# The prompt's values computed with the tokens on the output partitions, and first of all products

## The chip, the cores and the metric

The kernel runs on one core of one Trainium2 chip. The metric is the device time of one launch in microseconds; lower is better. Three runs of the kernel before were timed, and a fourth was profiled.

## The reference

One layer of a decoder step on two groups of tokens: a prompt of 512 new tokens and 8 running sequences of 4 tokens each (32 "sample" tokens, each sequence with 4096 cached positions in pages of 128). All arithmetic is fp32. Cut to what matters here:

```python
glu_a, glu_b, q, k, v, g_conv, g_att = jnp.split(x @ w_in, cuts, axis=-1)   # 512,512,512,512,512,1024,1024 columns
u = glu_a * sigmoid(glu_b)
c, new_conv = causal_depthwise_conv(u, past_conv, conv_w, conv_b)           # 31 taps, 512 channels
conv_out = silu(layer_norm(c)) @ w_conv_proj
o = stick_breaking_attention(q, concat(past_k, k), concat(past_v, v), ...)  # 8 heads of 64
mixed = (sigmoid(g_conv) * conv_out + sigmoid(g_att) * (o @ w_att_proj)) @ w_out
x = layer_norm(ALPHA * x + mixed)
# then a SwiGLU FFN, a gated per-layer embedding and a second layer_norm
return x, k, v, new_conv                                                    # k and v of all new tokens are outputs
```

## The kernel before

Activations lie channels first: `x` is 8 blocks of 128 channels by 544 tokens (512 of the prompt, 32 of the samples). Every fp32 operand of a product is split into a high and a low part (`split`, line 275: a rounded copy `xh` or `wh`, mostly by ScalarE, and the rest `xl` or `wl` by VectorE or GpSimd), and a product is three: high x high, low x high, high x low (`passes`, line 464). Weights come in units of 512 KB (`w_load`, line 340), 8 blocks of 128 x 128 each; a unit is split in two halves into four rotating buffers, so that a half can only be split when a half of four back has been used. The raw units of q and k (`FIRST`, line 1721) lie in slots of their own, since the sample tokens need them whole and early; all others share three rotating buffers `wr`.

The order of the work is not written by hand. `main` (line 1110) is the main stream of products; beside it run streams as Python generators: the loader and splitter of weights, the prefetch of cache pages on SP's queue (17 slots of 512 KB at most), the scores and sums over the cache (`scores`, `decode`, lines 673 and 694; 32 chunks, with tiles `kv`, `z`, `dz`, `dl`, `dp`, `av`), the prompt's attention (`pa_pair`, line 780; tiles `pa`, `pb`, 12 pairs), the depthwise convolution on VectorE (`conv`, line 868; 31 steps for each of four channel blocks, tile `c`, and sums over channels `tot`), and norms. A planner (`Weave`, line 64) with a clock for each engine decides at build time which stream issues next, by costs written in the code. What it emits is a fixed order for each engine, and on the chip each engine follows it strictly, waiting where an operand is late.

The main stream first goes through the 20 units of `ORDER` (line 1720): q, k, b, a, v of the first 128 output channels, then of the second, and so on. The weights are the stationary operand and x moves, so the result has channels on the partitions and tokens along the row. For q and k only the 512 prompt tokens move (one product of 512 columns); for b, a and v all 544 move as two products of 272. After b and a comes the gated `u`, which starts that block's convolution. v is the odd one: attention needs it with tokens on the partitions, so `vt` is copied out of PSUM (line 1209), stored, transposed in four 128 x 128 pieces by TensorE through the bank `tp` and copied to `v` by VectorE (`back`, line 1216), and then two more pieces with the samples' tokens go through the same bank to `vs` (`sample`, line 1224). The bank `tp` is shared with the transposes of the scores (`dz`), of the prompt's weights (`pa`) and with half of the prompt's scores. At the very start `first_sample` (line 1075) computes q and k of the 32 sample tokens from the raw units of `FIRST` (`z<-wq,xr`) and transposes them (`a_s`); `decode` then prepares the new tokens' part (`anew`), and only after that do the cache chunks start.

After the 20 units come the attention and convolution gates (`ga`, `gc`, 8 units each), the two projections (`ohl`, `sh`), the output projection (`m`) with the first norm in two halves of 256 tokens, and then the FFN; its second part, with 288 columns, needs the finished sample rows `r_s` that `sample_tail` (line 966) makes once all cache chunks are through.

Of the kernel before, what the change touches and what calls it, by code (L numbers as in the profile page):

```python
# [175 lines left out]
def step_kernel(ctx: ExitStack, tc: tile.TileContext, xT, pT, ck, cvv, state, pt, W, cv, cc, yT, kT, vT, cvo):  # L176
# [195 lines left out]
    def loader():  # L372
        for u in range(NU):
            if u in FIRST:
                continue
            if u in AGAIN:
                yield lambda: AGAIN[u] in kept
                raw[u] = kept.pop(AGAIN[u])
                continue
            if u in SLOTTED:  # L380
                yield lambda: u * 8 <= cur["pos"] + 8 * WAHEAD
            elif u in PAIR and u == PAIRS[PAIR[u]][1]:
                yield lambda: u * 8 <= cur["pos"] + 40 and cur["wp"] < 3
            else:
                yield lambda: u * 8 <= cur["pos"] + 32 and cur["raw"] < 3
            w_load(u)
# [307 lines left out]
    def decode():  # L694
        yield on(qblk, ks)
        for r in range(2):
# [17 lines left out]
            V.tensor_copy(out=anew[:, r, 112:128], in_=zb[:, :16])  # L714
# [65 lines left out]
    def pa_pair(idx, m, tiles):  # L780
# [55 lines left out]
        for i, c, w in seg:  # L836
            for kt in range(i + 1):
                for r, (zb, l) in zip(rows, ab):
                    mm(0.125, pa["o"][r, 128 * i:128 * i + 128], v_sb[m][:, kt * 128 + r.start:kt * 128 + r.stop],
                       l[:, c + kt * 128:c + (kt + 1) * 128], kt == 0, kt == i)  # L840
# [269 lines left out]
    def main():  # L1110
# [7 lines left out]
        raw[0] = slot("wq", (128, 1024))  # L1118
# [12 lines left out]
        for u in FIRST[1:]:  # L1131
# [4 lines left out]
        wv.add(first_sample(list(xr), dict(raw)), 2)  # L1136
# [35 lines left out]
        vs = v2 = None  # L1172
        wv.add(prompt_attention(), 2)
        wv.add(conv(), 3)
        for w, m in ORDER:
            o = []
# [29 lines left out]
            else:  # L1206
                yield spare(1)
                vt = tmp("vt")
                S.activation(out=halves(vt), in_=p[:, :, :HT], func=AF.Copy)
                wv.when(on(vt), lambda m=m, vt=vt: store(vT[m], vt))  # L1210
                if m % 2 == 0:
                    v2 = slot("v", (128, 2, 512))
                if m == 0:
                    vs = slot("vs", (128, 2, 512))

                def back(m=m, vt=vt, v2=v2):
                    yield wv.bank("tp")
                    tp = bank("tp")
                    for kt in range(4):
                        tr(tp[:, kt * 128:(kt + 1) * 128], vt[:, kt * 128:kt * 128 + 128])  # L1220
                    V.tensor_copy(out=v2[:, m % 2], in_=tp)
                    v_sb[m] = v2[:, m % 2]

                    def sample():
                        yield wv.bank("tp")
                        tp = bank("tp")
                        for r in range(2):
                            tr(tp[:, r * 128:(r + 1) * 128], vt[:, 400 + 16 * r:528 + 16 * r])
                        V.tensor_copy(out=vs[:, :, m * 128:(m + 1) * 128],
                                      in_=tp[:, :256].rearrange("p (r c) -> p r c", r=2))  # L1230
                        drop()
                        if m == 3:
                            v_sb["vs", 0], v_sb["vs", 1] = vs[:, 0], vs[:, 1]
                    wv.when(on(v2), sample)
                wv.when(on(vt), back)
# [484 lines left out]
ORDER = [(w, m) for m in range(4) for w in "qkbav"]  # L1720
# [13 lines left out]
def layout(d):  # L1734
# [15 lines left out]
    q, k, v = _units(wi[:, 1024:1536]), _units(wi[:, 1536:2048]), _units(wi[:, 2048:2560])  # L1750
# [31 lines left out]
OUTS = {"yT": (8, 128, 544), "kT": (4, 128, 544), "vT": (4, 128, 544), "cvo": (4, 128, 302)}  # L1782


def unlayout(r):
# [6 lines left out]
    vp, vs = tok(r["vT"])  # L1792
# [23 lines left out]
```

## Time and profile before

| | us |
|---|---|
| median of three runs | 994.26 |
| lowest, highest | 992.68, 996.72 |
| the profiled execution | 997.66 |
| its span | 995.9 |
| TensorE busy (products) | 950.5 (95%) |
| TensorE weight loads busy | 830.8 (83%) |
| VectorE busy | 782.9 (79%) |
| ScalarE busy | 538.5 (54%) |
| GpSimd busy | 177.7 (18%) |
| moved by DMA | 222.00 MB, mean 223 GB/s |

The engines are PE (TensorE), PEld (its weight loads), DVE (VectorE), ACT (ScalarE), POOL (GpSimd) and SP (the queue that issues nearly all loads). A line such as L238 or L146 is that of a helper through which all products or all vector operations go, so tiles are told apart by name: `g<-xh,wh` is a product into the bank `g` with `xh` moving and `wh` stationary. In a row that groups instructions stand the count, then the busy time in us, the mean ns of one, and the idle time of the engine just before them with what ended it. In a row in order of time stand the start and the duration in us. Busy time of a product covers its way through the array, so the spacing of starts, not the mean duration, says what one costs in a run of them.

### The profile page before, as it was taken

What the parts mean: (1) busy time and instruction counts of PE and PEld (TensorE: products, weight loads), DVE (VectorE), ACT (ScalarE), POOL (GpSimd) and SP (SyncE); (2) the same over time, 40 slices, a digit from 0 to 9 for tenths busy, and PEclk for the clock granted to TensorE, in tenths of its full rate; (3) what the DMA queues carried; (4) which work ended last, traced back from release to release, by engine and by line L of the source; (5) the groups of instructions that cost most, each with busy time, mean ns of one, the idle gap of its engine ahead of it and who ended that gap; (6) DMA issues with size and microseconds to landing.
All of it is one profiled execution on the core that took longest, in us unless ns stands there. A gap on an engine that the chain in (4) does not pass through costs nothing.

```text
span 995.9 us, 22464 instructions
## 1 busy us (share of the span) xinstructions
PE 950.5 (95%) x7998; PEld 830.8 (83%) x7998; DVE 782.9 (79%) x1287; ACT 538.5 (54%) x1041; POOL 177.7 (18%) x156
## 2 busy tenths in 40 slices
PE   8989998999899999999999879999999999999995
PEld 7866566668777797688878779999999999999994
DVE  4798898999965666466688786999999999943366
ACT  4634666576786786244467554554554555622224
POOL 1230323313111102033343240000000000220020
PEclk9999999999999999999999889999999999999997
DMA  9949999999979999999999634223223221222302
GB/s 356 343 158 305 339 309 333 316 318 313 328 257 322 314 347 345 331 335 356 321 324 369 248 109 178 96 86 117 96 86 126 87 85 65 86 105 85 128 1 90
DMA packets 101393, 222.00 MB, mean 223 GB/s; under 512 B 11169, under 2 KB 14498, under 8 KB 101282
## 3 DMA queue, kind: packets, MB, share of 16 engines
q1 hardware_dynamic: 99410, 217.46, 62.5%
q10 hardware_dynamic: 1872, 3.11, 0.8%
q8 instruction: 63, 1.03, 0.4%
q14 instruction: 48, 0.39, 0.1%
HBM read 215.45 MB, written 5.07 MB: 221 GB/s over the span
## 4 chain that ended last, share of the span: by engine, by line
PE 73%; DVE 14%; DMA 6%; issue 3%; ACT 2%; SPq 2%; POOL 0%; ACTq 0%; DVEq 0%; POOLq 0%
PE g L238 43%; PE z L238 10%; PE av L238 8%; PE o L238 5%; DVE c L146 5%; PE tp L238 4%; DMA kv<-in_ck 3%; DVE pb L146 2%; PE tp L243 1%; DMA wr<-in_W 1%; SPq L228 1%; DVE dl L146 1%; SPq L657 1%; DVE pa L146 1%; DVE dz L146 1%
## 5 line engine op out<-in xcount | busy, mean ns | idle before, releaser
L146 ACT ACTIVATE wh<-wr 128x512 fp32r<-128x512 f32 x236 | 147.0, 628 | 202.9 <-PE g L238 100.7
L146 DVE TENSOR_TENSOR wl<-wr,wh 128x512 fp32r<-128x512 f32 x190 | 133.1, 705 | 51.7 <-ACT wh L146 42.9
L146 POOL TENSOR_TENSOR wl<-wr,wh 128x512 fp32r<-128x512 f32 x50 | 82.0, 1645 | 493.8 <-ACT wh L146 455.7
L238 PE MATMUL g<-xh,wh 128*128 128x272 f32 (+1 forms) x512 | 127.4, 320 | 0.6 <-ACT wh L146 0.6
L238 PE MATMUL g<-h,wh 128*128 128x272 f32 x704 | 122.3, 290 | 0.0
L238 PE MATMUL g<-xl,wh 128*128 128x272 f32 (+1 forms) x512 | 119.3, 305 | 0.8 <-DVE xl L146 0.8
L238 PE MATMUL g<-xh,wl 128*128 128x272 f32 (+1 forms) x512 | 119.1, 304 | 0.7 <-POOL wl L146 0.7
L146 DVE SCALAR_TENSOR_TENSOR c<-u,cvt,c 128x512 f32<-128x512 f32 x120 | 113.1, 943 | 3.3
L238 PEld LDWEIGHTS g<-h,wh 128*128 128x128 f32 x704 | 103.1, 189 | 0.3
L238 PEld LDWEIGHTS g<-xh,wh 128*128 128x128 f32 x512 | 83.3, 192 | 22.3 <-issue 17.8
L238 PEld LDWEIGHTS g<-xl,wh 128*128 128x128 f32 x512 | 83.7, 191 | 3.6 <-DVE xl L146 1.5
L238 PEld LDWEIGHTS g<-xh,wl 128*128 128x128 f32 x512 | 83.3, 191 | 3.7 <-POOL wl L146 1.0
L238 PE MATMUL g<-h,wl 128*128 128x272 f32 x352 | 80.1, 289 | 0.0
L146 ACT ACTIVATE wh<-wq 128x512 fp32r<-128x512 f32 x87 | 54.5, 629 | 39.6 <-PE g L238 28.7
L238 PE MATMUL g<-x1h,wh 128*128 128x272 f32 (+2 forms) x216 | 65.0, 301 | 5.4 <-ACT x1h L146 4.8
L238 PE MATMUL z<-kv,qblk 128*32 128x256 f32 x1024 | 65.5, 382 | 2.6 <-DMA kv<-in_ck 2.6
L238 PE MATMUL g<-x1h,wl 128*128 128x272 f32 (+2 forms) x216 | 63.4, 294 | 0.0
L238 PE MATMUL g<-x1l,wh 128*128 128x272 f32 (+2 forms) x216 | 63.4, 293 | 0.0
L146 DVE TENSOR_TENSOR wl<-wq,wh 128x512 fp32r<-128x512 f32 x75 | 54.7, 734 | 10.9 <-ACT wh L146 9.8
L238 PE MATMUL av<-kv,dp 128*32 128x512 f32 x512 | 63.2, 608 | 0.0
L146 ACT ACTIVATE pa<-pa 128x384 f32<-128x384 f32 (+1 forms) x96 | 52.5, 555 | 17.3 <-DVE pa L146 15.8
L238 PEld LDWEIGHTS g<-h,wl 128*128 128x128 f32 x352 | 58.1, 188 | 0.0
(316 smaller groups left out, 2352.1 us busy)
## 6 DMA issues: line engine op xcount, KB each, us to landing
kv<-in_ck SPq DMA_DIRECT2D x256, 256.0 KB, 4.4
kv<-in_cvv SPq DMA_DIRECT2D x256, 256.0 KB, 5.3
wr<-in_W SPq DMA_DIRECT2D x98, 512.0 KB, 3.9
wq<-in_W SPq DMA_DIRECT2D x37, 512.0 KB, 5.0
wa<-in_W SPq DMA_DIRECT2D x12, 512.0 KB, 10.2
xr<-in_xT SPq DMA_DIRECT2D x8, 272.0 KB, 5.0
out_yT<-pw SPq DMA_DIRECT2D x6, 272.0 KB, 2.3
out_kT<-qk ACTq DMA_DIRECT2D x4, 272.0 KB, 5.5
```

What stands on the lines that cost most here:

```text
L146: fn(**kw)
L228: eng.dma_start(out=out, in_=in_)
L238: T.matmul(out, lhsT=lhsT, rhs=rhs, start=start, stop=stop)
L243: T.transpose(out, in_, ident)
L657: reg[col] = nc.sync.value_load(ptt[0:1, col:col + 1], min_val=0, max_val=POOL - 1)
```

## The change

The values leave the shared loop and get a function of their own, `values`. There the roles are exchanged: for each of the 8 channel blocks, x is the stationary operand (128 channels by 128 tokens) and the weights move (512 columns, all value channels at once). Five accumulations run side by side, four for the prompt's 512 tokens and one for the last 128 tokens, of which 32 are the samples' and 96 the prompt's again; they take both double banks `g` and the bank `o`. The results have tokens on the partitions and are copied out of PSUM as they are, by VectorE or ScalarE (`evac`), and stored; there are no transposes and no `vt`. The output array's layout and its reading back change with it, and so do the places where the samples' own weights stand in `anew` (96 + 16 r in place of 112).

`ORDER` now has the four value units first, then b, a, q, k for each channel block. So the first unit comes through the shared buffers `wr`, the next two are loaded ahead of q and k, and the fourth, b0 and a0 behind them.

```diff
-            if u in FIRST:
+            if u in FIRST or u < 3:
...
-            V.tensor_copy(out=anew[:, r, 112:128], in_=zb[:, :16])
+            V.tensor_copy(out=anew[:, r, 96 + 16 * r:112 + 16 * r], in_=zb[:, :16])
...
-                    mm(0.125, pa["o"][r, 128 * i:128 * i + 128], v_sb[m][:, kt * 128 + r.start:kt * 128 + r.stop],
+                    mm(0.125, pa["o"][r, 128 * i:128 * i + 128], v_sb[m][kt][:, m * 128 + r.start:m * 128 + r.stop],
...
-        raw[0] = slot("wq", (128, 1024))
+        raw[0] = big.tile([128, 1024], F32, tag="wr", bufs=3, name="wr")
+        cur["raw"] += 1
...
-        for u in FIRST[1:]:
+        for u in (1, 2, *FIRST):
             w_load(u)
...
-        vs = v2 = None
+        def values():
+
+            yield room()
+            p = [gps()]
+            yield room()
+            p.append(gps())
+            yield wv.bank("o")
+            out = [p[t // 2][:, t % 2] for t in range(4)] + [bank("o")]
+            cols = [slice(128 * t, 128 * t + 128) for t in range(4)] + [slice(NT - 128, NT)]
...
+            for k in range(8):
...
+                w, x = hl[divmod(pos // 4, 2)], xin(k)
+                yield on(*w, *x)
+                for t in range(5):
+                    for i, (a, b) in enumerate(((x[0], w[0]), (x[1], w[0]), (x[0], w[1]))):
+                        mm(0.2305, out[t], a[:, cols[t]], b, k == 0 and i == 0, k == 7 and i == 2)
+                    yield
...
+            v = [slot("v", (128, 2, 512)) for i in range(2)] + [slot("vs", (128, 512))]
+            v = [v[t // 2][:, t % 2] for t in range(4)] + [v[2]]
+            for t in range(5):
+                evac(v[t], out[t])
...
         for w, m in ORDER:
+            if w == "v":
+                if m == 0:
+                    yield from values()
+                continue
...
-                vt = tmp("vt")
-                S.activation(out=halves(vt), in_=p[:, :, :HT], func=AF.Copy)
-                wv.when(on(vt), lambda m=m, vt=vt: store(vT[m], vt))
...
-                def back(m=m, vt=vt, v2=v2):
-                    yield wv.bank("tp")
-                    tp = bank("tp")
-                    for kt in range(4):
-                        tr(tp[:, kt * 128:(kt + 1) * 128], vt[:, kt * 128:kt * 128 + 128])
-                    V.tensor_copy(out=v2[:, m % 2], in_=tp)
...
-ORDER = [(w, m) for m in range(4) for w in "qkbav"]
+ORDER = [("v", m) for m in range(4)] + [(w, m) for m in range(4) for w in "baqk"]
...
-OUTS = {"yT": (8, 128, 544), "kT": (4, 128, 544), "vT": (4, 128, 544), "cvo": (4, 128, 302)}
+OUTS = {"yT": (8, 128, 544), "kT": (4, 128, 544), "vT": (5, 128, 512), "cvo": (4, 128, 302)}
```

How this moves instructions is told by the order on each engine. First TensorE at the place where the first cache scores (`z<-kv`) stand. Before, they come in b1, the eighth unit (`g_955`), behind q1 and k1 (`g_903`) and behind the first block's value transposes:

```order
L243 MATMUL tp_941<-cct_65,anew_73 128x128
L238 MATMUL g_903<-xh_132,wh_817 128x512
L238 MATMUL g_903<-xl_133,wh_817 128x512
L238 MATMUL g_903<-xh_132,wl_818 128x512
L238 MATMUL g_955<-xh_126,wh_851 128x272 x2
L238 MATMUL g_955<-xl_127,wh_851 128x272 x2
L238 MATMUL g_955<-xh_126,wl_852 128x272 x2
L238 MATMUL z_963<-kv_134,qblk_68 32x256
```

Now, in b0 (`g_664`), the first unit behind the values:

```order
L243 MATMUL tp_710<-cct_65,anew_73 128x128
L238 MATMUL g_664<-xh_136,wh_490 128x272 x2
L238 MATMUL g_664<-xl_137,wh_490 128x272 x2
L238 MATMUL g_664<-xh_136,wl_491 128x272 x2
L238 MATMUL g_664<-xh_138,wh_490 128x272 x2
L238 MATMUL g_664<-xl_139,wh_490 128x272 x2
L238 MATMUL g_664<-xh_138,wl_491 128x272 x2
L238 MATMUL z_727<-kv_140,qblk_68 32x256
```

The cache scores have moved from the eighth unit of the main stream to the one that follows the values; ahead of them stand the values' 120 products and most of b0 in place of q0, k0, b0, a0, v0, q1 and k1.

Second VectorE at the start of the convolution (`c`). Before, in its first channel block, the copies of the transposed values stand between its steps:

```order
L146 COPY v_823<-tp_869 128x512
L146 SCALAR_TENSOR_TENSOR c_135<-u_538,cvt_64,c_135 128x512 x4
L146 COPY vs_824<-tp_912 128x2x128
L146 SCALAR_TENSOR_TENSOR c_135<-u_538,cvt_64,c_135 128x512 x4
L146 COPY anew_73<-tp_941 128x128
```

Now the same block begins behind a0's gate (`u`), with the scan chain of a cache chunk (`dp`, `dl`, `dz`, `cnew`) in that place:

```order
L146 TENSOR_TENSOR u_764<-g_773,sg_767 128x8x4
L146 TENSOR_SCALAR c_141<-u_764,cvt_64 128x512
L146 SCALAR_TENSOR_TENSOR c_141<-u_764,cvt_64,c_141 128x512 x3
L146 TENSOR_SCALAR dp_985<-dz_799 128x256
L146 SCALAR_TENSOR_TENSOR dl_800<-dl_800,cnew_74,dp_985 128x256
L146 TENSOR_TENSOR dz_799<-dz_799,dl_800 128x256
L146 COPY cnew_74<-dl_800 128x1
L146 SCALAR_TENSOR_TENSOR c_141<-u_764,cvt_64,c_141 128x512 x14
```

The copies out of `tp` are gone from among the steps, `anew` is finished ahead of the convolution, and the first two chunks' scans now stand ahead of it or just behind its first steps.

Third TensorE in the first FFN part, at the last of the sample tokens' sums (`sq_s`) and the first product that needs the finished sample rows (288 columns). Before, 12 products stand between the two, of which these are the last:

```order
L238 MATMUL g_9373<-x1h_8536,wh_9317 128x256
L238 MATMUL g_9373<-x1l_8537,wh_9317 128x256
L238 MATMUL g_9373<-x1h_8536,wl_9318 128x256
L238 MATMUL g_9446<-x1h_8396,wh_9339 128x288
L238 MATMUL g_9446<-x1l_8397,wh_9339 128x288
```

Now the sample tail's last sum stands in the embedding's products (`ph`, `pl`), ahead of six units of 256 columns:

```order
L238 MATMUL g_8995<-pl_8694,wh_8873 128x272 x2
L238 MATMUL g_8995<-ph_8693,wl_8874 128x272 x2
L238 MATMUL av_9003<-sq_s_8908,on_m_67 128x32
L238 MATMUL g_8995<-ph_8693,wh_8873 128x272 x2
L238 MATMUL g_8995<-pl_8694,wh_8873 128x272 x2
```

Between that sum and the first product of 288 columns there are now 18 products of 272 columns and 144 of 256. In the same region the second half's norm sum (`o<-ln`) has moved into the sample tail's output projection (`z<-wa,m_s`).

More of the change, by code (lines that the diff above doesn't have):

```diff
@@ L1135, in main @@
         nc.gpsimd.memset(eps, EPS)
-        wv.add(first_sample(list(xr), dict(raw)), 2)
+        wv.add(first_sample(list(xr), {u: raw[u] for u in FIRST}), 2)
         wv.add(prefetch(), 0)
@@ L1170, in glu, with rest @@
             store(cvo[i], u[:, 512:814])
-        vs = v2 = None
+        def values():
[6 more added lines that the diff above has]
+            cols = [slice(128 * t, 128 * t + 128) for t in range(4)] + [slice(NT - 128, NT)]
+            base = cur["next"]
+            cur["next"] += 32
+            for k in range(8):
+                pos = base + 4 * k
+                cur["pos"] = max(cur["pos"], pos)
+                yield lambda: ("w", *divmod(pos // 4, 2)) in flag and xin(k) is not None
+                w, x = hl[divmod(pos // 4, 2)], xin(k)
[4 more added lines that the diff above has]
+                    yield
+                del w, x, a, b
+                used(pos + 3)
+            v = [slot("v", (128, 2, 512)) for i in range(2)] + [slot("vs", (128, 512))]
+            v = [v[t // 2][:, t % 2] for t in range(4)] + [v[2]]
+            for t in range(5):
+                evac(v[t], out[t])
+            def rest():
+                for t in range(5):
+                    yield on(v[t])
+                    store(vT[t], v[t])
+                for m in range(4):
+                    v_sb[m] = v[:4]
+                v_sb["vs", 0] = v_sb["vs", 1] = v[4]
+            wv.add(rest(), 0)
         wv.add(prompt_attention(), 2)
@@ L1205, in main @@
                 sg = None
-            else:
-                yield spare(1)
-                vt = tmp("vt")
-                S.activation(out=halves(vt), in_=p[:, :, :HT], func=AF.Copy)
-                wv.when(on(vt), lambda m=m, vt=vt: store(vT[m], vt))
[L1211 to L1214, printed above, removed]
-                def back(m=m, vt=vt, v2=v2):
-                    yield wv.bank("tp")
-                    tp = bank("tp")
-                    for kt in range(4):
-                        tr(tp[:, kt * 128:(kt + 1) * 128], vt[:, kt * 128:kt * 128 + 128])
-                    V.tensor_copy(out=v2[:, m % 2], in_=tp)
[L1222 to L1235, printed above, removed]
         ga = []
@@ L1749, in layout @@
     ug, uu = _units(up[:, :2816]), _units(up[:, 2816:])
-    q, k, v = _units(wi[:, 1024:1536]), _units(wi[:, 1536:2048]), _units(wi[:, 2048:2560])
+    q, k = _units(wi[:, 1024:1536]), _units(wi[:, 1536:2048])
+    v = wi[:, 2048:2560].reshape(4, 2, 128, 512).transpose(0, 2, 1, 3).reshape(4, 128, 1024)
     W = [{"q": q, "k": k, "v": v, "a": a, "b": b}[w][m:m + 1] for w, m in ORDER]
@@ L1791, in unlayout @@
     kp, ks = tok(r["kT"])
-    vp, vs = tok(r["vT"])
+    vp, vs = r["vT"][:4].reshape(512, 512), r["vT"][4, 96:]
     c = r["cvo"].reshape(512, 302)
```

## The prediction

> **What bounds the kernel now.** I read the page first, then busy time by stages, then what each engine waited for, then the groups of instructions, and last single rows in order of time. The profiled execution took 997.66 us, 1.8 more than its span; it lies 3.4 us (0.34%) above the median of the three runs shown, 994.26. Every sum below is a difference against this execution, and I put the difference on the median. About 0.5%, 5 us, is what a measurement of this kernel can tell from no change.
>
> The stages, cut where the depthwise convolution begins and ends on VectorE and at the last long wait of TensorE:
>
> ```profile
> span 995.9 us, 22464 instructions
> 0.00:43.30 43.30, 39.95 (x399) 34.44 (x400) 23.00 (x50) 22.07 (x41) 9.39 (x18) 1.00 0.96 356
> 43.30:267.30 224.00, 206.25 (x1721) 152.87 (x1719) 207.77 (x332) 137.53 (x285) 62.45 (x56) 0.97 0.89 301
> 267.30:574.10 306.80, 300.52 (x2724) 241.58 (x2724) 206.88 (x334) 188.05 (x382) 71.76 (x64) 0.99 0.91 322
> 574.10:587.50 13.40, 8.61 (x49) 8.26 (x48) 12.96 (x32) 8.18 (x19) 6.97 (x4) 0.75 0.23 79
> 587.50:995.90 408.40, 395.15 (x3111) 393.66 (x3110) 332.31 (x543) 182.70 (x317) 27.08 (x15) 0.99 0.27 97
> ```
>
> After the times and the stage's length come PE, PEld, DVE, ACT and POOL busy, then the granted clock, the DMA share and GB/s. TensorE is the bound outside the second stage. In the second it idles 17.8 us, and VectorE is as busy as it (207.8 of 224). What TensorE waited for in the whole span, with VectorE's own waits between 43 and 267 us behind it:
>
> ```profile
> PE tp L243 <- ACT pa L146: 7.6, 5, 2.5
> PE tp L243 <- DVE v L146: 6.5, 3, 4.4
> PE g L238 <- ACT x1h L146: 4.8, 1, 4.8
> ```
> ```profile
> DVE wl L146 <- ACT wh L146: 5.1, 3, 3.2
> DVE dp L146 <- PE av L238: 2.7, 2, 1.6
> DVE dp L146 <- ACT pa L146: 1.1, 1, 1.1
> ```
>
> The 6.5 us are the transposes of the values, held up because an earlier copy of a transposed bank sits in VectorE's queue between convolution steps. VectorE itself waits only 8.9 us in the stage; so convolution, scans and copies set when it ends:
>
> ```profile
> 43.26 0.53 DVE L146 TENSOR_SCALAR c<-u,cvt 128x512 f32<-128x512 f32 x1
> 266.50 0.73 DVE L146 TENSOR_TENSOR tot<-tot,c 128x544 f32<-128x544 f32 x1
> 267.28 0.72 PE L238 MATMUL o<-tot,on_m 128*128 128x272 f32 x2 [0.66 <-DVE tot L146]
> ```
>
> TensorE stands at the sum over channels until VectorE has delivered it. That is the joint at which I compare the two kernels.
>
> **The change, part by part: TensorE's work.** The spacing of long products is read from the first and the last row of a run of 40, that of 272-column pairs from a run of 23:
>
> ```profile
> 6.23 0.50 PE L238 MATMUL g<-xh,wh 128*128 128x512 f32 x1 [0.60 <-ACT wh L146]
> 10.27 0.39 PE L238 MATMUL g<-xh,wl 128*128 128x512 f32 x1
> ...
> 19.33 0.40 PE L238 MATMUL g<-xh,wl 128*128 128x512 f32 x1
> 19.66 3.70 PE L238 MATMUL z<-wq,xr 128*32 128x128 f32 x128
> 33.64 0.41 PE L238 MATMUL g<-xl,wh 128*128 128x272 f32 x2
> ...
> 39.15 0.41 PE L238 MATMUL g<-xh,wl 128*128 128x272 f32 x2
> ```
> ```profile
> L243 PE MATMUL tp<-cct,vt 128*128 128x128 f32 x24 | 4.5, 299 | 6.5 <-DVE v L146 6.5
> L238 PE MATMUL z<-kv,qblk 128*32 128x256 f32 x1024 | 65.5, 382 | 2.6 <-DMA kv<-in_ck 2.6
> ```
>
> (19.33 - 10.27) / 39 = 0.2323 us for 512 columns; (39.15 - 33.64) / 22 = 0.2505 for a pair, 0.1252 for one. Removed: 4 units x 8 blocks x 3 products x 2 halves = 192 x 0.1252 = 24.0 us and 24 transposes, 4.5: 28.5. Added: 8 blocks x 5 token tiles x 3 = 120 x 0.2323 = 27.9. The fifth tile computes 96 prompt tokens a second time, which is why so little is saved: 0.6 us, all in stages where something else ends last, so nothing.
>
> The step of 0.2323 already contains the loading of the stationary operand, which goes on beside the products. The Trainium skill, "TensorE: Matmul & The Clock Gate", section "The mechanism" (Part 3), says that such loads overlap with running products only where the row groups differ, and here they do not; by that the 72 loads saved would count in full (a rival below). The trace disagrees: one product starts 0.2323 us after another although the load between them is itself about 0.19 us.
>
> ```profile
> L238 PEld LDWEIGHTS g<-xh,wh 128*128 128x128 f32 x512 | 83.3, 192 | 22.3 <-issue 17.8
> ```
>
> **When the convolution starts.** It needs b0 and a0, which now stand behind the values, the queries of the samples and two chunks of scores. TensorE: 6.23 for the first product; 1.4 of the 2.3 us that the first 48 products lost to arriving x (19.66 - 6.23 - 48 x 0.2323), since each block of x now feeds 15 products in place of 3; 27.9 values; 3.7 for the sample projection, at which I count no wait (its last weights land behind three more units of 512 KB, 4.4 us at the 356 GB/s of the first stage, but TensorE arrives there 5.4 us later, at 6.23 + 1.4 + 75 x 0.2323 = 25.1 in place of 19.66); about 2.7 for the small transposes, masks and the wait for the query block, an estimate; 96 x 0.1252 = 12.0 for b0 and a0; 2 x 2.05 (65.5 / 32 chunks) = 4.1 for scores. Sum 58.0; with the gate's products 59. Before it was 43.3, so the start is 15.7 us later.
>
> **What VectorE no longer does in that stretch.** By the order of the two kernels, between the first convolution step and the last channel sum these leave: four v copies, four vs copies, six of twelve wl subtractions, one chunk's scan chain (it now runs ahead of the convolution), one ohl subtraction and two sigmoid additions.
>
> ```profile
> L146 DVE COPY v<-tp 128x512 f32<-128x512 f32 x4 | 2.7, 682 | 0.0
> L146 DVE COPY vs<-tp 128x256 f32<-128x256 f32 x4 | 1.7, 416 | 0.0
> L146 DVE TENSOR_TENSOR wl<-wr,wh 128x512 fp32r<-128x512 f32 x190 | 133.1, 705 | 51.7 <-ACT wh L146 42.9 <-PE z L238 7.7
> L146 DVE TENSOR_TENSOR_SCAN dl<-dl,cnew,dp 128x256 f32<-128x256 f32 x32 | 26.2, 818 | 6.6 <-ACT dl L146 4.7
> L146 DVE TENSOR_TENSOR dz<-dz,dl 128x256 f32<-128x256 f32 x32 | 18.4, 575 | 1.1
> L146 DVE TENSOR_SCALAR dp<-dz 128x256 f32<-128x256 f32 x32 | 12.0, 376 | 11.5 <-ACT dz L146 7.1 <-PE av L238 3.2 <-ACT pa L146 1.1
> ```
>
> 2.7 + 1.7 + 6 x 0.705 + (0.818 + 0.575 + 0.376) + 3 x 0.7 (priced as wl) = 12.5 us. The five evacuations that replace the copies run before the convolution, partly on ScalarE. The stretch was 207.8 busy, 8.9 waiting and 7.3 between instructions. After: 195.3 + 7.3 = 202.6 with no wait, 211.5 with all of them. From 59 the sum over channels comes at 261.6 to 270.5, against 267.3. VectorE starts later and lags TensorE more, so its waits should shrink by half: 266; and TensorE reaches the last scan's transposes late, with some products still between them and the sum: I take 267, **no gain here**. The 6.5 us of waits on the value copies do go, but what is late next is the same VectorE queue, through the scans and pa chains that the 7.6 us row names.
>
> **After the joint.** The first chunk of cache scores moves ahead by some 15 us:
>
> ```profile
> 64.78 1.93 PE L238 MATMUL z<-kv,qblk 128*32 128x256 f32 x32
> ```
> ```profile
> SPq L228 <- PE z L238: 13.9, 3, 13.1
> ```
>
> Before, SP stood 13.1 us with all cache slots full until that first score; now the slots free in time and the cache stream is one chunk ahead from there on, so decoding ends earlier in TensorE's order. That reaches the wait of 4.8 us. Behind the last sample sum (sq_s) stood 12 products of 256 columns before the first that needs the finished sample rows; now 18 of 272 and 144 of 256:
>
> ```profile
> 572.66 0.28 PE L238 MATMUL g<-x1l,wh 128*128 128x256 f32 x1
> 573.83 0.28 PE L238 MATMUL g<-x1h,wl 128*128 128x256 f32 x1
> 578.90 0.61 PE L238 MATMUL g<-x1h,wh 128*128 128x288 f32 x1 [4.79 <-ACT x1h L146]
> ```
>
> At 0.117 us each (1.17 / 10) that is 19 us of cover for a chain of some 6.7 (the sum runs at 572.2), so the wait goes. With it goes its echo: the fourth stage holds 48 products, 6.0 us at the 0.1252 of the 272-column ones, but lasts 13.4 at a granted clock of 0.75. **Gain 7.4.** The Trainium skill, same page, section "HAM oscillation — how this bites in real kernels", has the clock fall back to half after an idle gap over about 3.4 us; one such window would cost 1.7 us on top of the 4.8, an estimate of 6.5 in all by that page, and the sum below would be -2.5. The trace agrees that the clock falls; its price is larger.
>
> A new wait appears. Between the two sums of the second norm (o<-tot, o<-ln) stood a long run of products; now 18 of 256 columns, a transpose and 80 sample products.
>
> ```profile
> 524.56 0.70 PE L238 MATMUL o<-tot,on_m 128*128 128x256 f32 x2
> 534.16 1.14 DVE L146 TENSOR_TENSOR ln<-ln 128x512 f32<-128x512 f32 x2
> L238 PE MATMUL z<-wa,m_s 128*32 128x128 f32 x128 | 3.9, 274 | 0.0
> ```
>
> The chain took 535.3 - 525.3 = 10.0 us; the cover is 18 x 0.117 + 0.4 + 80 x 0.061 (3.9 / 64) = 7.4. Cost 0 to 5.6 (the difference, and slow clock after it as above): I take 2.5, the plain difference. All of TensorE's queue stands behind it.
>
> The cache stream has to deliver its last 16 chunks some 5 us sooner than before, at a DMA share that was 0.91; before, TensorE waited 2.6 us for it in all (the row of z<-kv above). Cost 0 to 5, nearest to that row: 1.5. On SP the loads of the fourth value unit, of b0 and of a0 wait for the three shared buffers, which the splits of the first three units free at about 17 us (two blocks of products after the start, 14.6, and the last split), and the cache loads queue behind them; the units of q and k are still on their way until about 24 us (19.66 + 4.4), so this costs nothing, and a few us of the new lead if that cover were gone. The value stores (five of 256 KB on ScalarE's queue, where four of 272 KB were) wait for nothing that is late.
>
> **Sum.** 0 - 7.4 + 2.5 + 1.5 = -3.4 us: 994.3 on the profile's scale, 990.9 on the median's.
>
> **The rivals.** (1) *VectorE's waits vanish and the norm wait does not arise*: the joint at 261.6, -5.7; -7.4; +1.5: -11.6, 982.7. For it: its waits came from an empty queue. Against: TensorE and VectorE feed each other in that stage. (2) *The late convolution decides*: if all VectorE waits stay, the stretch of 211.5 is late as soon as it starts after 55.8 (267.3 - 211.5). Started at 63, if the sample projection or the decode preparation holds TensorE 4 us more than I count, the joint is at 274.5, +7.2; with the new norm wait at its upper price, -7.4 + 5.6 + 1.5: +6.9, 1001.2. For it: VectorE is idle 20.3 of the first 43.3 us and will now be idle longer. (3) *The cache stream takes it back*: waits of 5 instead of 1.5: about 994.4. For it: the DMA engines are 0.9 busy up to 574 us. (4) *Weight loads are not hidden*, and 192 - 120 = 72 fewer of them shorten TensorE's queue: 72 x 0.192 = 13.8 less than the forecast, 977. Against it: the step of 0.2323.
>
> **Chances.** Forecast 0.46 (987 to 996 by its own bounds, a third of it below 989.3); (1) 0.25; (2) 0.17; (3) 0.10; (4) 0.02. Faster by over 0.5%: 0.15 + 0.25 + 0.02 = 0.42; within: 0.31 + 0.10 = 0.41; slower 0.17. The range 981 to 1001 leaves out (4) and the outer parts of (1) and (2), some 0.17.
>
> **What would show it.** First convolution step at 57 to 62 us; the sum over channels near 267; no row of values waiting for transposes; SP's wait of 13 us gone; first cache score before 50 us; the row x1h at the 288-column products gone, and a wait of a few us at o<-ln instead. Wrong, if the sum over channels is off by more than 5 us, if the x1h wait stays, or if waits on kv grow past 5 us.

## The result, and the profile after

The changed kernel takes 1018.7 us in the median of six runs (1014.96 to 1020.39), the kernel before beside it 993.89 (six runs, 992.68 to 996.72): a ratio of 1.0235, 95% interval 1.0217 to 1.0254. It is 2.3% slower, where 990.9 us was forecast and 1001 was the upper end.

Its profile has less work than before on TensorE's weight loads and on VectorE, more busy time on TensorE (954.4 us in place of 950.5), and a longer span:

```profile
span 1017.4 us, 22264 instructions
PE 954.4 (94%) x7902; PEld 822.6 (81%) x7902; DVE 779.3 (77%) x1274; ACT 538.9 (53%) x1041; POOL 174.3 (17%) x162
```

First the rows that answer to those of the prediction. The convolution's first step and the end of the sum over channels on VectorE, and the products that wait for it on TensorE:

```profile
65.25 1.12 DVE L146 TENSOR_SCALAR c<-u,cvt 128x512 f32<-128x512 f32 x1
274.51 0.72 DVE L146 TENSOR_TENSOR tot<-tot,c 128x544 f32<-128x544 f32 x1
282.89 0.73 PE L238 MATMUL o<-tot,on_m 128*128 128x272 f32 x2
```

The convolution starts at 65.3 us in place of the forecast 59, the sum is there at 275.2 in place of 267, and TensorE takes it up 7.7 us after that, without waiting for it: TensorE itself is late. What it waited for in the whole span:

```profile
PE tp L243 <- ACT pa L146: 17.3, 9, 4.9
PE g L238 <- DVE sg L146: 8.7, 4, 3.4
PE tp L243 <- ACT dp L146: 5.0, 2, 4.5
PE av L238 <- DVE sq_s L146: 4.7, 2, 2.6
PE z L238 <- ACT dz L146: 3.2, 1, 3.2
PE g L238 <- DVE m L146: 2.0, 1, 2.0
```

The 6.5 us for copies of the values and the 4.8 for x1h are gone, as forecast. The 2.6 for cache pages are gone too, where 1.5 more had been forecast. The wait for the chains of the prompt's attention (`tp` for `pa`) has grown from 7.6 to 17.3 us, and the waits for `sg`, `dp` and `sq_s` are new or larger.

To see where this counts, both spans are cut at three points that stand in the same order on TensorE in both kernels: the first product of the attention projection (`ohl`), the first on the normed rows (`x1h`, 256 columns) and the first of the token sums (`z` from `x1h`). I call the stages A to D. Before, and then after (columns as in the prediction):

```profile
0.00:386.82 386.82, 364.21 (x3186) 283.35 (x3187) 303.34 (x493) 248.95 (x500) 84.34 (x82) 0.98 0.91 312
386.82:522.16 135.34, 133.56 (x1129) 104.03 (x1127) 92.68 (x145) 63.77 (x130) 43.19 (x42) 1.00 0.95 333
522.16:614.50 92.34, 83.25 (x771) 75.19 (x769) 72.57 (x137) 55.75 (x119) 28.41 (x22) 0.93 0.64 238
614.50:995.90 381.40, 369.45 (x2920) 368.23 (x2918) 314.32 (x514) 170.05 (x294) 21.71 (x11) 0.99 0.25 90
```
```profile
0.00:407.72 407.72, 375.05 (x3191) 278.01 (x3191) 301.03 (x487) 252.29 (x508) 91.10 (x87) 0.97 0.91 313
407.72:544.86 137.14, 133.60 (x1106) 103.69 (x1103) 90.10 (x148) 62.97 (x129) 36.36 (x38) 0.99 0.95 337
544.86:636.09 91.23, 76.26 (x694) 72.68 (x693) 74.25 (x126) 53.47 (x112) 24.86 (x26) 0.94 0.43 157
636.09:1017.40 381.31, 369.44 (x2920) 368.23 (x2918) 313.88 (x514) 170.15 (x294) 21.92 (x11) 0.99 0.25 90
```

Length less the first busy time is TensorE's idle time: A 22.6 before and 32.7 after, B 1.8 and 3.5, C 9.1 and 15.0, D the same. Stage A is 20.9 us longer. 10.1 of these are idle time. Some 8.0 are decoding done earlier: the cache products in A are 1040 before and 1136 after, 64 more for scores at 0.064 us (65.5 / 1024) and 32 more sums at 0.123 (63.2 us for 512 on the profile's page of the kernel before). The other 2.8 are about what the lower granted clock (0.97 in place of 0.98) makes of the busy time. That decoding is paid back in C, where TensorE has 7.0 us less to do (83.25 less 76.26), but C is only 1.1 shorter, because 5.9 us more of it are idle. So the loss of 21.5 in the span is 17.7 of idle time in A, B and C (10.1, 1.7, 5.9) and some 3 to 4 at a lower clock (TensorE's busy time is 3.9 us more). The experiments ask where these waits come from.

### The profile page after: what moved, and what is told of

Its sections match the earlier page's. It is cut to its first block, busy times and chain, and to the rows that moved or that the text cites. A ratio compares the mean times of both kernels' runs of the same rounds, so it can differ in the third digit from the quotient of the medians.

```text
span 1017.4 us, 22264 instructions
## 1 busy us (share of the span) xinstructions
PE 954.4 (94%) x7902; PEld 822.6 (81%) x7902; DVE 779.3 (77%) x1274; ACT 538.9 (53%) x1041; POOL 174.3 (17%) x162
## 4 chain that ended last, share of the span: by engine, by line
PE 71%; DVE 10%; DMA 9%; SPq 4%; issue 3%; ACT 3%; POOL 0%; DVEq 0%; ACTq 0%; POOLq 0%
PE g L238 41%; PE z L238 10%; PE av L238 9%; PE o L238 5%; PE tp L238 4%; DMA kv<-in_cvv 3%; SPq L228 3%; DVE c L146 2%; DMA wr<-in_W 2%; DMA kv<-in_ck 1%; SPq L657 1%; PE tp L243 1%; DVE pb L146 1%; DMA xr<-in_xT 1%; DVE tw L146 1%
## 5 line engine op out<-in xcount | busy, mean ns | idle before, releaser
L146 ACT ACTIVATE wh<-wr 128x512 fp32r<-128x512 f32 x233 | 144.6, 628 | 211.5 <-PE g L238 94.4
L146 POOL TENSOR_TENSOR wl<-wr,wh 128x512 fp32r<-128x512 f32 x47 | 75.2, 1603 | 481.0 <-DVE pw L146 262.7
L238 PE MATMUL g<-xh,wh 128*128 128x272 f32 (+1 forms) x448 | 113.0, 322 | 0.1
L146 DVE SCALAR_TENSOR_TENSOR c<-u,cvt,c 128x512 f32<-128x512 f32 x120 | 104.2, 868 | 3.5
L238 PE MATMUL g<-xh,wl 128*128 128x272 f32 (+1 forms) x448 | 104.9, 304 | 0.0
L238 PE MATMUL g<-xl,wh 128*128 128x272 f32 (+1 forms) x448 | 104.6, 303 | 0.0
L238 PEld LDWEIGHTS g<-xh,wh 128*128 128x128 f32 x448 | 72.0, 189 | 26.4 <-issue 22.4
L238 PEld LDWEIGHTS g<-xh,wl 128*128 128x128 f32 x448 | 72.2, 189 | 2.9
L238 PEld LDWEIGHTS g<-xl,wh 128*128 128x128 f32 x448 | 72.5, 189 | 1.7
L146 DVE TENSOR_TENSOR wl<-wq,wh 128x512 fp32r<-128x512 f32 x74 | 51.8, 706 | 20.5 <-ACT wh L146 20.3
## 6 DMA issues: line engine op xcount, KB each, us to landing
xr<-in_xT SPq DMA_DIRECT2D x8, 272.0 KB, 5.7
out_yT<-pw SPq DMA_DIRECT2D x6, 272.0 KB, 2.2
out_kT<-qk ACTq DMA_DIRECT2D x4, 272.0 KB, 5.4
```

The lines of the kernel that those rows point to most:

```text
L146: fn(**kw)
L238: T.matmul(out, lhsT=lhsT, rhs=rhs, start=start, stop=stop)
```

## The experiments

Four theories stood at the start. **A**: the five value stores, issued back to back, hold ScalarE's queue. **B**: the convolution starts late, and VectorE, full from there on, ends late. **C**: the new form of the values costs by itself. **D**: a planner's constants were fitted to the old order. Two more came out of the first results. **E**: decoding, which covers TensorE's waits, is used up before stage C. **F**: scans of the attention are queued behind convolution steps that the planner issues ahead on VectorE.

All results stand in one table. Times are in us. "Convolution" is the start of its first step and "sum" the start of the last addition of the sum over channels (it ends some 0.7 us later). A stage is given as its length / TensorE's idle time. "Scans" is the row `tp` for `pa` of TensorE's waits: transposes that wait for a bank which the chains of the prompt's attention hold. The profiles are one execution each, up to 4 us off the median of their kernel, so a us or two between two stages says little. "Lead" and "held" are explained at e5 to e7.

| kernel | ratio to before, 95% | convolution | sum | A | B | C | scans |
|---|---|---|---|---|---|---|---|
| before | 1 | 43.3 | 266.5 | 386.8 / 22.6 | 135.3 / 1.8 | 92.3 / 9.1 | 7.6 |
| changed | 1.0235 (1.0217 to 1.0254) | 65.3 | 274.5 | 407.7 / 32.7 | 137.1 / 3.5 | 91.2 / 15.0 | 17.3 |
| e1 stores on SyncE | 1.0203 (1.0164 to 1.0242) | 60.3 | 272.0 | 406.5 / 28.9 | 136.7 / 3.5 | 90.4 / 14.2 | 16.0 |
| e2 old form, first | 1.0088 (1.0054 to 1.0121) | 57.5 | 273.8 | 394.2 / 24.1 | 138.9 / 5.1 | 91.2 / 12.4 | 14.3 |
| e3 new form, later | 1.0163 (1.0130 to 1.0196) | 43.5 | 312.7 | 402.6 / 30.5 | 134.8 / 2.5 | 88.1 / 10.1 | 17.5 |
| e4 b0, a0 first | 1.0303 (1.0282 to 1.0323) | 28.5 | 274.0 | 409.5 / 34.0 | 138.6 / 4.7 | 91.7 / 13.0 | 6.7 |
| e5 e1, scores held | 1.0130 (1.0100 to 1.0161) | 59.2 | 272.6 | 406.1 / 29.4 | 126.4 / 3.5 | 91.7 / 8.1 | 17.0 |
| e6 before, lead 1.5 | 1.0038 (1.0016 to 1.0059) | 43.4 | 284.3 | 385.0 / 18.0 | 134.5 / 2.6 | 95.9 / 12.6 | 3.2 |
| e7 e1, lead 1.5 | 1.0086 (1.0057 to 1.0114) | 60.2 | 299.6 | 391.4 / 18.7 | 134.8 / 3.8 | 91.8 / 13.3 | 7.6 |
| e8 e1, lead 1.5, held | 0.9974 (0.9957 to 0.9992) | 60.8 | 297.4 | 388.7 / 18.2 | 129.7 / 3.2 | 91.8 / 8.2 | 9.3 |
| e9 e2, lead 1.5 | 1.0012 (0.9995 to 1.0030) | 56.9 | 301.7 | 380.9 / 16.9 | 141.8 / 7.6 | 88.1 / 11.2 | 12.4 |
| e10 e1, lead 1.0, held | 0.9913 (0.9894 to 0.9931) | 60.0 | 341.5 | 383.5 / 14.4 | 129.7 / 2.7 | 91.8 / 8.1 | 0.4 |
| e11 e6, held | 1.0022 (1.0001 to 1.0042) | 43.4 | 285.1 | 386.1 / 18.8 | 137.7 / 4.3 | 93.8 / 12.5 | 3.4 |
| e12 before, lead 1.0 | 0.9924 (0.9909 to 0.9939) | 43.6 | 311.5 | 381.1 / 17.3 | 136.1 / 2.9 | 91.3 / 9.5 | 2.1 |
| e13 e10, stores on ScalarE | 0.9964 (0.9946 to 0.9982) | 62.2 | 342.2 | 384.0 / 15.1 | 130.2 / 2.9 | 90.2 / 7.9 | none |
| e14 e2, lead 1.0, held | 1.0005 (0.9985 to 1.0026) | 57.7 | 318.2 | 388.3 / 21.0 | 130.0 / 2.7 | 91.6 / 7.9 | 3.3 |

Stage D is 381.3 to 381.4 us in all sixteen.

**The stores (e1).** In the changed kernel ScalarE's queue stands still from 44 to 54 us, and VectorE with it:

```profile
43.53 0.35 ACTq L233 DMA_DIRECT2D out_vT<-v  x1
44.83 5.22 ACTq L233 DMA_DIRECT2D out_vT<-v  x3
53.59 0.34 ACTq L233 DMA_DIRECT2D out_vT<-vs  x1
53.97 0.63 ACT L146 ACTIVATE wh<-wq 128x512 fp32r<-128x512 f32 x1 [10.13 <-DMA out_vT<-v]
```
```profile
54.63 0.69 DVE L146 TENSOR_TENSOR wl<-wq,wh 128x512 fp32r<-128x512 f32 x1 [9.99 <-ACT wh L146]
```

In the trace the 700 transfers signal eight semaphores (a semaphore is a counter that an engine can wait for), 87 or 88 transfers each, whichever queue they are on. Each of the first four stores is issued 0.07 to 0.08 us after the earlier transfer on its own semaphore, a cache load of SP's, has landed: the landings are at 43.45, 44.76, 47.04 and 49.64 us, the stores at 43.53, 44.83, 47.12 and 49.71. (For the fifth the trace has no landing.) So five stores in a row wait for one landing after another, and everything behind them on ScalarE stands.

```diff
-                    store(vT[t], v[t])
+                    nc.sync.dma_start(out=vT[t], in_=v[t])
+                    moved(v[t])
```

> The changed kernel with its five value stores on SyncE's queue in place of ScalarE's; nothing else is altered. Theory A (the five stores, issued back to back, hold ScalarE's queue for 10 us and so delay the start of the convolution from 59 to 65 us, and with it the rest): first convolution step at 56 to 60 us, sum over channels 5 to 9 us earlier than the 275.2 of the changed kernel, time 1008 to 1013 us if 6 to 10 us of it go on to the end, 994 if the stores are all of the loss. Theory B (the order of the products, with the values first and the convolution late, costs it whatever ScalarE does): first convolution step earlier by up to 6 us, but time 1014 us or more. Theory C (the form of the values, x stationary, costs it): 1017 to 1020.

1016.63 us (1012.83 to 1017.22), ratio 1.0203. The convolution starts at 60.3, and the sum over channels comes 2.5 us earlier, not 5 to 9; A has 3.8 us less idle time, the span ends 2.6 earlier. The time lies in theory B's range (1014 or more) and outside A's, and the intervals of 1.0203 and 1.0235 overlap. So the stores explain 5 us of the late start, but at most a small part of the loss. The Trainium skill, "DMA: Bandwidth & Descriptors", section "Issuing engines are not separate DMA queues", says that issuing on several engines saves only sequencer time and that this is usually small; here the place of five issues held an engine for 10 us, though little of it reached the end of the kernel.

**The order alone (e2), the form alone (e3).** e2 is the kernel before with the new `ORDER`, `raw[0]` and loader. e3 is the changed kernel with

```diff
-ORDER = [("v", m) for m in range(4)] + [(w, m) for m in range(4) for w in "baqk"]
+ORDER = [(w, 0) for w in "qkba"] + [("v", m) for m in range(4)] + [(w, m) for m in range(1, 4) for w in "qkba"]
```

> The values in the old form (weights stationary, transposed behind), but as the first of all products, and the products in the order b, a, q, k behind them, as in the changed kernel: order alone. Theory A (stores): the four stores are 6 us apart, ScalarE's queue isn't held, first convolution step at 59 to 61, time 994 to 1000. Theory B (order): 1012 to 1020. Theory C (form): 994, as the kernel before.

> The values in the new form (x stationary, five accumulations, no transposes), but behind q0, k0, b0 and a0, and the other heads' products in the order q, k, b, a: form alone, with the convolution started early. Theory A (stores): first convolution step near 43, ScalarE's queue held some 10 us near 75 us in the middle of the convolution, time 995 to 1005. Theory B (order): first step near 43, time 985 to 995. Theory C (form): 1012 or more.

e2: 1004.37 us (1003.46 to 1007.57), ratio 1.0088, between the forecasts of A and B. e3: 1011.28 (1008.6 to 1012.08), 1.0163, between A and C. None of the three holds alone: the place costs 0.9%, and in that place the new form, with its stores on SyncE, costs 1.1% more (1.0203 against 1.0088). In e3 the convolution starts as early as before, its sum comes 46 us later, and the kernel is still faster than the changed one. That is the first sign that neither the start nor the sum over channels says what a kernel takes.

**Early convolution (e4), held scores (e5), another lead (e6, e7).** e4 and e5 stand on e1. `CAHEAD` (line 1717 of the changed kernel) is the lead: how far, in us of the planner's time, convolution steps (and, later, those of the residual `rr`) may be issued ahead on VectorE. e5 holds the scores of the last five cache chunks back until the first half of the output projection is done.

```diff
e4
-ORDER = [("v", m) for m in range(4)] + [(w, m) for m in range(4) for w in "baqk"]
+ORDER = [("b", 0), ("a", 0)] + [("v", m) for m in range(4)] + [("q", 0), ("k", 0)] + [(w, m) for m in range(1, 4) for w in "baqk"]
e5, in scores()
+            if c == 27:
+                yield done("woA")
e6 and e7
-CAHEAD = 2.5
+CAHEAD = 1.5
```

> The new form of the values with its stores on SyncE's queue, but b0 and a0 as the very first products and the values behind them (then q0, k0, then b, a, q, k of the other heads): the convolution starts early. Theory B (the late start of the convolution is what costs: VectorE is full from its start to the sum over channels): first convolution step at 25 to 35 us, TensorE's idle time up to the first product of the attention projection 20 to 25 us (before 22.6, the stores-on-SyncE kernel 28.9), time 990 to 1000 us. Theory C (the form itself costs 10 us, wherever the convolution starts): idle 28 to 33, time 1005 to 1015. Theory D (the plan's constants were fitted to the old order, any other order costs some 10 us): 1003 to 1012.

> The changed kernel with its stores on SyncE's queue, and the scores of the last five cache chunks (27 to 31) held back until the first half of the output projection is done, so that decoding is again left over for the second norm and the first part of the feed-forward. Theory E (the change uses up the decoding, which is TensorE's filler, earlier, and so leaves the waits of that part uncovered): TensorE idle between the first product on the normed rows and the first product of the token sums falls from 14.2 us to 8 to 10, time 1009 to 1012 us against 1014 to 1017. Rival (the work is only moved, and the wait of 4.8 us for the finished sample rows comes back with its slow clock): idle there 10 to 15, time as without it, 1013 to 1018.

> The kernel before with one constant of its planner altered (the convolution may be issued 1.5 us ahead on VectorE, not 2.5): the same work in another interleaving. Theory D (constants fitted to the old order): 999 to 1005 us, and TensorE idle up to the first product of the attention projection 26 to 30 us in place of 22.6. Theories B and C: 993 to 998 us, as before.

> The changed kernel with its stores on SyncE's queue and the same constant at 1.5: another interleaving of the changed kernel. Theory D: anything from 1003 to 1015 us, not tied to the 1016.6 of its own default; fitted anew it could come back to 1005. Theories B and C: 1013 to 1018.

e4: 1024.14 us (1022.81 to 1025.78), the slowest of all, with the earliest convolution (28.5 us). B falls, and C and D foretold too little as well. The wait for scans is down to 6.7, but others stand in its place:

```profile
PE z L238 <- DMA kv<-in_ck: 9.8, 10, 2.2
PE g L238 <- DVE sg L146: 8.4, 5, 4.7
PE tp L243 <- ACT pa L146: 6.7, 3, 3.4
PE g L238 <- DVE u L146: 5.9, 1, 5.9
PE g L238 <- ACT v L146: 3.9, 1, 3.9
```

e5: 1007.02 us (1005.41 to 1010.56), 1.0130 against e1's 1.0203, a little more than E foretold. Stage C is 1.4 us longer than in e1, but holds 7.5 us more work and 6.1 less idle time; that work has left stage B, which is 10.2 us shorter:

```profile
406.09:532.52 126.43, 122.98 (x1014) 100.40 (x1011) 87.95 (x145) 59.57 (x120) 30.89 (x34) 1.00 0.95 331
532.52:624.24 91.72, 83.59 (x787) 74.54 (x786) 76.20 (x142) 55.98 (x119) 19.61 (x19) 0.96 0.58 207
```

This shows E: in the changed kernel the same cache products, done earlier, no longer lie in the waits of C (for the sample rows' sums `sq_s` and the gates `sg`).

e6: 998.0 us (995.44 to 999.88), 1.0038: the old order loses little with this lead, so D in the form expected (999 to 1005, A's idle time up) fails; A's idle time even falls to 18.0, while C's rises to 12.6. e7: 1001.75 us (1001.11 to 1005.8), 1.0086 in place of e1's 1.0203, faster than every theory had it. Stage A is 15.1 us shorter, 10.2 of it idle time, and the wait for scans is down from 16.0 to 7.6 (e7's stage A):

```profile
0.00:391.37 391.37, 372.71 (x3159) 277.91 (x3159) 300.99 (x487) 251.39 (x508) 85.76 (x85) 0.99 0.94 324
```
This is F; it was put up on this result, and e8 and e10 are its tests. How it works is read from the longest of these waits in the changed kernel, on TensorE, ScalarE and VectorE:

```profile
111.55 0.40 PE L238 MATMUL g<-xh,wl 128*128 128x512 f32 x1
116.84 0.69 PE L243 MATMUL tp<-cct,dz 128*128 128x128 f32 x2 [4.89 <-ACT pa L146]
117.18 0.78 PE L238 MATMUL g<-xh,wh 128*128 128x512 f32 x1
117.75 0.63 PE L238 MATMUL g<-xl,wh 128*128 128x512 f32 x1
118.18 0.63 PE L238 MATMUL g<-xh,wl 128*128 128x512 f32 x1
118.74 0.48 PE L238 MATMUL o<-pa,v 128*64 128x128 f32 x2
```
```profile
109.48 0.47 ACT L146 ACTIVATE pa<-tp 128x384 f32<-128x384 f32 x1
113.62 0.52 ACT L146 ACTIVATE pa<-pa 128x384 f32<-128x384 f32 x1 [3.67 <-DVE pa L146]
116.00 0.42 ACT L146 ACTIVATE dz<-dz 128x256 f32<-128x256 f32 x1 [1.85 <-DVE dz L146]
116.32 0.47 ACT L146 ACTIVATE pa<-tp 128x384 f32<-128x384 f32 x1
```
```profile
108.42 0.87 DVE L146 TENSOR_TENSOR cs<-u,cvt 128x124 f32<-128x124 f32 x4
109.33 0.67 DVE L146 TENSOR_REDUCE c<-cs 128x16 f32<-128x496 f32 x1
109.91 1.76 DVE L146 TENSOR_TENSOR cs<-u,cvt 128x124 f32<-128x124 f32 x4
111.59 0.34 DVE L146 TENSOR_SCALAR pb<-pa 128x384 f32<-128x384 f32 x1
112.04 0.96 DVE L146 TENSOR_TENSOR_SCAN pb<-pb,pa 128x384 f32<-128x384 f32 x1
113.03 0.56 DVE L146 TENSOR_TENSOR pa<-pa,pb 128x384 f32<-128x384 f32 x1
113.51 0.66 DVE L146 TENSOR_REDUCE c<-cs 128x16 f32<-128x496 f32 x1
114.20 0.24 DVE L146 TENSOR_SCALAR c<-c,cvt 128x32 f32<-128x32 f32 x1
...
115.54 0.42 DVE L146 TENSOR_TENSOR dz<-dz,dl 128x256 f32<-128x256 f32 x1
```

TensorE wants bank `tp` for a cache chunk's transposes. ScalarE empties it at 116.32, and stands until then behind two exponentials whose inputs VectorE delivers at 113.6 and 116.0. VectorE has no wait there: the chain for the first begins at 111.59 behind 3.2 us of convolution (108.42 to 111.6), the one for the second after another 0.9 (from 113.51). While TensorE waits, all products behind the transposes stand too. The three products after the wait start 0.43 to 0.57 us before the next one, not 0.2323, and the granted clock is 0.64 from 116.84 to 121.20: the slow clock that the prediction saw behind the x1h wait, now in stage A. The Trainium skill, "TensorE: Matmul & The Clock Gate", section "HAM oscillation — how this bites in real kernels", has the clock fall behind idle gaps over about 3.4 us; the gap here is 4.9, and the trace agrees. But shorter waits do it too. The second chunk of cache scores comes behind a wait of 3.19 us and takes twice as long as the first (granted clock 0.54 from 55.02 to 58.76):

```profile
48.19 1.93 PE L238 MATMUL z<-kv,qblk 128*32 128x256 f32 x32
55.02 3.82 PE L238 MATMUL z<-kv,qblk 128*32 128x256 f32 x32 [3.19 <-ACT dz L146]
```

In the kernel before, the granted clock is 0.50 from 200.82 to 204.20 us, just behind a wait of 2.46 us for `pa`. So the short waits of this kernel also have a price in clock.

**The cures together (e8 to e11).** e8 is e7 with e5's hold; e9 is e2 with a lead of 1.5; e10 is e8 with a lead of 1.0; e11 is e6 with the hold.

> The changed kernel with its stores on SyncE's queue, the planner's lead of the convolution at 1.5 us and the last five chunks of scores held back: the three cures together. If scans behind convolution steps (theory F) and used-up decoding (theory E) are separate losses that add: 0.86% less 0.73% above before, 993 to 998 us against some 994 to 995, TensorE idle 18 to 20 up to the attention projection and 8 to 10 in the first part of the feed-forward. If they are one loss seen twice: 1000 to 1004.

> The values first in the old form (with transposes), lead of the convolution 1.5 us: the old form beside the new one in the same interleaving rule. Theory C (the form costs by itself some 11 us more than the old one in the same place, as 1016.6 against 1004.4 at 2.5): 990 to 995. Theory F (what the form cost was scans queued behind convolution steps, an accident of the lead of 2.5): 998 to 1005, as the 1001.8 of the new form.

> As the three cures together, with the lead at 1.0 us. Theory F with a longer reach (the shorter the lead, the fewer steps a scan waits for): 2 to 5 us faster than at 1.5, TensorE idle up to the attention projection 14 to 18. Rival (VectorE runs dry between the steps, the convolution ends later still and the gain turns): 2 to 8 us slower than at 1.5.

> The kernel before with the lead at 1.5 us and the last five chunks of scores held back: the same two cures without the change. Theory E in general (left-over decoding covers the waits of the feed-forward in any kernel): idle there from 12.6 to 8 or 9, 992 to 996 us. Rival (before the change enough decoding is left there anyway): 996 to 1000.

e8: 993.57 us (990.45 to 997.0), ratio 0.9974, inside the first forecast: what lead and hold cure are separate losses that add up (the hold is worth 0.7% at a lead of 2.5 and 1.1% at 1.5). e9: 997.09 (993.18 to 1001.22), 1.0012, in neither range, and nearer to F's than to C's; the old form is 0.7% faster than the new one with the same lead in e7. e10: 988.14 (985.66 to 991.19), 0.9913. The shortest lead tried is the best, with the sum over channels at 341.5, 67 us later than in the changed kernel, nearly no wait for scans (0.4), and the granted clock in stage A at 1.00 in place of 0.97. The largest wait that is left is for cache pages (stage A, then that wait):

```profile
0.00:383.50 383.50, 369.14 (x3140) 277.19 (x3141) 286.62 (x487) 242.87 (x493) 64.55 (x73) 1.00 0.95 328
```
```profile
PE z L238 <- DMA kv<-in_ck: 9.6, 9, 2.0
```

The row for scans alone does not rank the kernels: e4 has 6.7 and is the slowest, e9 has 12.4 and is level with the kernel before.

e11: 997.4 (995.1 to 1006.83), 1.0022 against e6's 1.0038. The hold does nothing for the old order, whose decoding ends later by itself: the rival was right there.

**Is it the change, or the lead (e12 to e14)?** e12 is the kernel before with `CAHEAD = 1.0`; e13 is e10 with the stores back on ScalarE's queue; e14 is e2 with a lead of 1.0 and the hold.

> The kernel before with the lead of the convolution at 1.0 us, nothing else altered. If the gain of the shorter lead belongs to the new order alone (scans there queue behind convolution steps because prompt attention begins under a running convolution): 995 to 1000, ratio 1.000 to 1.005, as at 1.5. If it is a gain of any order: 984 to 990, as much below before as the changed kernel with all cures.

> The changed kernel with the lead at 1.0 us and the scores held, but its five value stores back on ScalarE's queue: what they cost in an interleaving without the other losses. Theory A in its small form (the convolution starts 5 us later and part of it goes on): ratio 0.3 to 0.6% above the 0.9913 of the same with stores on SyncE, 991 to 994. Rival (the hold of ScalarE is covered by TensorE's products there, only VectorE's start moves): 0.990 to 0.993, 986 to 989.

> The values first in the old form (transposes; stores spread by themselves on ScalarE), lead 1.0 us, scores held: the old form with the same cures. Theory C (the form is worth something either way): more than 0.5% from 0.9913. Theory F (form counts for nothing, 28.5 us against 27.9 on TensorE, once the scans are not queued): 0.987 to 0.996.

e12: 988.17 us (986.43 to 991.94), 0.9924: at 1.0 us the short lead is a gain for the old order too, inside the second forecast, though at 1.5 it had cost 0.4% (e6). The intervals of e12 and of e10 (0.9913) overlap for the most part: with the lead at 1.0, the change is worth nothing that can be measured, even with its stores moved and its scores held. Not run were the kernel before with both the lead of 1.0 and the hold, the changed kernel at 1.0 without the hold, and any lead below 1.0. e13: 991.64 (986.76 to 996.64), 0.9964, above e10's by 0.5% and clear of its interval, as theory A's small form foretold: on ScalarE's queue the stores cost about half a percent here. Where it goes is not shown, for the execution that was profiled is one of the fastest (987.61 us): its span is that of e10 (985.8 against 986.4), with ScalarE held 8.5 us and no stage longer by over 0.6 us. e14: 995.34 (992.01 to 1001.51), 1.0005, as theory C had it and outside F's range: here the old form is 0.9% slower than the new one in e10 (0.4% slower than e13, whose stores are on ScalarE as well), where at 1.5 without the hold it was 0.7% faster and at 2.5 1.1% faster. The form has no price of its own that keeps its sign; what it is worth depends on how the planner interleaves the work around it.

## Why the prediction was wrong

Its sum has -3.4 us; the span grew by 21.5. Its small terms were right; it failed at the joint and in what decoding was worth.

- **TensorE's work, 28.5 out and 27.9 in: right as far as the rows show.** b0 begins at 42.64 us, where the terms of the prediction up to it give 41.9 (6.23 + 1.4 + 27.9 + 3.7 + 2.7).
- **Start of the convolution, 59: off by 6.3**, because "the value stores ... wait for nothing that is late" looked at what the stores wait for and not at what waits behind them on ScalarE. Without them the start is 60.3 (e1). This is the step that the prediction should have priced, though little of it came through to the end.
- **The stretch to the sum over channels, 202.6 to 211.5: inside its bounds by luck**, 210.0 (65.25 to 275.23). VectorE's waits there shrank to 2.6 us from 8.9, more than the half that was taken, but its busy time fell from 207.8 to 199.6 only, not to 195.3: two errors that nearly cancel. The sum is there 8 us later than the 267 of the forecast, and most of that is the late start. By the prediction's own sign (more than 5 us off) that alone made it wrong.
- **The joint at that sum, "no gain here": this step failed.** TensorE was taken to be bound there, on a wait of 0.66 us, and neutral elsewhere in the stage. In e6, e7, e10 and e12 the sum comes 18 to 75 us later than before, and e10 and e12 are faster than before. TensorE has other products to put ahead of it; what it cannot pass is a wait in its own order. Those waits, the scans' transposes, stood in the prediction's own row (7.6 us) and were named as "what is late next", but no growth of theirs was priced beyond the 6.5 us that went. They became 17.3, with 3.9 us more for `dp`. Net of the 6.5 us, TensorE idles 10.1 us more in stage A, and the slow clock behind such waits makes up about the other 2.8 of its loss; the remaining 8.0 are moved work.
- **After the joint, -7.4: this step failed too. What it says of decoding came, the gain did not.** The score before 50 us (48.19), SP's wait for it gone (13.9 in all before, 1.5 now) and the x1h wait gone came as written, and the decoding did move ahead by about 8 us. But the moved work was itself the cover of stage C, which got 1.1 us shorter with 7.0 us less to do. The prediction counted the wait that decoding would end and not those that it had hidden (`sq_s` 4.7, `sg` 8.7).
- **The new wait at o<-ln, 2.5, and at the cache stream, 1.5:** neither came; the changed kernel has no row of either. A wait of 2.0 for `m` is new. Rival (3), the cache stream, had no part in the changed kernel; its wait shows in e4 (9.8) and, once the other waits are cured, in e10 (9.6).
- **Rival (2)** had the right side and nearly its own numbers (start 63 and joint 274.5 against 65.3 and 275.2), but its start was late for another reason (ScalarE's queue, not TensorE), and its reason for the loss is one that the runs refute: lateness of the convolution is not the price (e3, e4, e10). Its near hit is luck.

Why TensorE waits more for scans in the changed order at the same lead is argued, not shown: 28 us of value products, which lay between the attention's steps before, now all lie ahead of the convolution, so TensorE has less to do while VectorE does nearly the same. From the first convolution step until TensorE takes up the sum over channels it was busy 206.25 of 224 us before and is 191.80 of 217.6 now. e2, e3 and e4, which also put the values in one block, lose as well at that lead. But in e3 the values stand behind the first convolution step, and its row for scans is 17.5 all the same, so this can't be the whole of it; and no run kept the new form spread out. That cause stays open.

## What to carry to other kernels

A point that one engine reaches late is a joint only if the other has nothing else to do there: sum its idle time by stages cut in its own order, and price every short wait that stands in that order, with the slow clock behind it. Work that is moved ahead takes its cover with it, so look up which waits it lay in before. A change of order in a kernel with a planner has to be timed at more than one setting of the planner's lead: here the lead alone cost the old kernel 0.4% at 1.5 and gained it 0.8% at 1.0, and the change, with its stores moved and its scores held, went from 2.3% slower to level with it.

## What the hardware showed that was not expected

A relu of 384 columns on VectorE took 0.35 us at one place and 1.51 us at another, where it began in the middle of a subtraction of GpSimd's (GpSimd's row and VectorE's, changed kernel):

```profile
97.31 1.74 POOL L146 TENSOR_TENSOR wl<-wq,wh 128x512 fp32r<-128x512 f32 x1
```
```profile
97.83 1.51 DVE L146 TENSOR_SCALAR pb<-pa 128x384 f32<-128x384 f32 x1
101.84 0.35 DVE L146 TENSOR_SCALAR pb<-pa 128x384 f32<-128x384 f32 x1
```

97.83 + 1.51 is 0.29 us after GpSimd's end at 99.05. The Trainium skill, "SBUF — State Buffer", section "SBUF: two separate sides", has the two engines share a pair of ports that one holds for a whole instruction while the other stands; these rows agree. In stage A of e10 GpSimd is busy 64.6 us and VectorE 286.6, in the changed kernel 91.1 and 301.0, VectorE for the same 487 instructions, GpSimd for 73 in place of 87; that this is the same lock was not tried.
